# Two layers of a hybrid encoder on one core: where a block's products with the states and the norm's sums stand on TensorE

## The chip, the cores and the metric

The kernel runs on one core of a Trainium2 chip. The metric is the device time of one execution in microseconds (us). A core has TensorE (PE, matrix products; PEld is its weight load), VectorE (DVE), ScalarE (ACT), GpSimd (POOL) and SyncE (SP, which issues nearly all transfers here). They run side by side, each takes its own instructions in order, and they wait for one another through semaphores.

## The reference, cut to what matters

Two layers are computed one after the other on a sequence of 512 tokens of width 1024. In each layer three branches read the same input: a state-space branch (SSD) that runs in both directions, a differential attention, and a cross-attention to 256 memory tokens. Their results are gated, merged, projected, and normalised with the residual. The edit lies in the state-space branch:

```python
def _ssd_scan(xs, a, bm, cm):              # one direction, chunks of 128 tokens
    a_cum = jnp.cumsum(a, axis=-1)
    decay = jnp.exp(jnp.where(lower, seg, -jnp.inf))          # seg = a_cum[q] - a_cum[s]
    y_diag = jnp.einsum('bcqgn,bcsgn,bgrcqs,bcsgrp->bcqgrp', cm, bm, decay, xs)
    states = jnp.einsum('bcqgn,bgrcq,bcqgrp->bcgrpn', bm, decay_states, xs)
    ...                                    # prev: the states carried from chunk to chunk
    y_off = jnp.einsum('bcqgn,bcgrpn,bgrcq->bcqgrp', cm, prev, jnp.exp(a_cum))
    return (y_diag + y_off).reshape(Bsz, L, H, P)
...
    y = y_fwd + y_bwd + d_skip.astype(jnp.float32)[:, None] * xs
    y = y.reshape(Bsz, L, SSD_INNER) * jax.nn.silu(z.astype(jnp.float32))
    return _rmsnorm(y, norm_w)             # over all 2048 channels of a token
```

There are 32 heads of 64 channels in 4 groups of 8 heads, and 4 chunks. A head's output has a part from within its chunk (`y_diag`) and a part from the states of earlier (backwards: later) chunks (`y_off`). The norm needs the sum of squares over all channels of a token, so over all groups.

## The kernel before, in words

**Units of weights.** All weights lie in memory as units of 128x1024 numbers. The list `plan` holds steps, each with or without a unit. `emit` goes through it: for a step with a unit it loads a unit some steps ahead (`wr`, two buffers, issued on SP), ACT rounds it to the short float format (`wh`, three buffers), DVE takes the rest (`wl`), and `proj` multiplies it in 24 matmuls (`mm3`: three for each of eight input tiles) into one bank `pj`. The input's two parts are `xh` and `xl`.

**The state-space branch, `ssd`.** For each group `g` of 8 heads: `bpart` and `cpart` project and convolve B and C (`bC`, `cC`) and form `gs`, the products of B and C within each chunk; four times `xpart` does so for the inputs (`xsC`, and transposed `xsT`); `states` forms the states `prev` carried between the chunks, in both directions. Then come four blocks `b`, each of two heads: `zpart` (a projection, the gate `sz`) and `ypart`. After the first group the `wpart` units, which multiply a group's result `yh`, `yl` with the branch's output weights and add it into `mrg` (`br` in the code), stand among the next group's `xpart` steps; those of the last group follow at the end. Some gates of the other branches are computed ahead between the blocks (`AHEAD`, tile `tg`).

**One block, `ypart`.** In this order it issues
1. two loads of `eb` (the exponentials of the summed decays, spread over the partitions) on SP, two buffers;
2. the products of the states with C for both directions, 6 matmuls `pm<-cC,prev` (12 records in the trace) into two banks `pm`, and on DVE their multiplication into `eb` (`eb<-pm,eb`, two of 128x384);
3. for each of its two heads: a load of `ab` (512 KB, two buffers), a minimum with the mask on DVE, eight exponentials on ACT, a sum on DVE, and the product with `gs`, which gives `m` (three buffers);
4. the products within the chunk, 8 matmuls `pm<-m,xsT` (16 records) into a bank `pm` called `py`;
5. on DVE `y` (first `y<-xsC,pr,pm`, then two additions of `eb`, then the product with `sz`), `yh` on ACT, `yl` on DVE, the square on ACT, and its addition into `sqa` on POOL.

**The order on each engine.** A planner goes through the program as it is written and gives each instruction a number that counts up; on each engine the instruction with the lowest number that it holds to be ready goes next, by its own model of durations. Two helpers change that. Inside `manual_schedule(engines={PE})` PE's instructions keep their written order among themselves, while others may still go between. `late(n)` adds `n` to the number of what stands inside (`late(-n)` takes `n` off), and what is inside doesn't count for what comes after. The first of the 8 matmuls of step 4 stands under `late(LD)`, the others under `late(-LD)` with `LD` = 80: the set is held back by 80 instructions, and once its first matmul has gone, the others follow at once. Tiles of one tag are given out in the order of the program; `pm` has 4 banks.

**The end of the branch.** `gpart(j)` projects the gates of this branch (tiles `th` and `sz`), three of them ahead; `norm` sums `sqa` over the partitions by four matmuls with one column each (`pt<-cst,sqa`, 8 records), takes the reciprocal root on DVE in small steps, spreads it by four matmuls (`pm<-cst,rs_y`), and ACT copies it into `rB`. The four `wpart(3, u)` follow, and then `fin(j)` multiplies gate, `rB` and `mrg`. In the code:

```python
            if j == 1:
                self.T(norm)
        for u in range(4):
            self.T(wpart(3, u), (l, UBS + 12 + u))
```

Of the kernel before, what the change touches and what calls it, by code (L numbers as in the profile page):

```python
# [15 lines left out]
ALU = mybir.AluOpType  # L16
# [4 lines left out]
P = 128  # L21
# [23 lines left out]
LX, LD, LN = 70, 80, 300  # L45
# [6 lines left out]
def bc(ap, shape):  # L52
    return ap.broadcast_to(shape)


class Net:
# [389 lines left out]
    def ssd(self, l):  # L446
# [85 lines left out]
        def ypart(g, b):  # L532
            def f():
                sp = self.sp
                if b == 0:
                    self.yh = self.t(sp, [P, 4, S], "yh", F32R)
                    self.yl = self.t(sp, [P, 4, S], "yl", F32R)

                eb = self.t(sp, [P, 2, S], "eb", bufs=2)
                for hh in range(2):  # L540
                    h = g * 8 + 2 * b + hh
                    src = self.deb.rearrange("(d h) q -> h d q", d=2)[h:h + 1]
                    nc.sync.dma_start(out=eb[hh * 64:(hh + 1) * 64], in_=src.broadcast_to([64, 2, S]))
                for d, cs in ((0, (1, 2, 3)), (1, (0, 1, 2))):
                    ps = self.bank(self.pm, "pm")
                    for c in cs:
                        q = slice(c * P, (c + 1) * P)
                        self.mm(ps[:, q], self.prev[d, c][:, b * P:(b + 1) * P], self.cC[:, q])
                    q = slice(cs[0] * P, (cs[2] + 1) * P)
                    self.tt(eb[:, d, q], ps[:, q], eb[:, d, q], ALU.mult)  # L550

                py = self.bank(self.pm, "pm")
                ms = []
                for hh in range(2):
                    h = g * 8 + 2 * b + hh
                    ab = self.t(sp, [P, 2, 4, P], "ab", bufs=2)
                    src = self.dab.rearrange("(d h) q -> h d q", d=2)[h:h + 1]
                    nc.sync.dma_start(out=ab.rearrange("p d c q -> p d (c q)"), in_=src.broadcast_to([P, 2, S]))

                    self.tt(ab, ab, bc(self.msk[:, :, None, :], [P, 2, 4, P]), ALU.min)  # L560
                    for d in range(2):
                        for c in range(4):
                            j = 32 * d + h
                            self.act(ab[:, d, c, :], ab[:, d, c, :], AF.Exp, bias=self.bias[:, c, j:j + 1])
                    self.tt(ab[:, 0], ab[:, 0], ab[:, 1], ALU.add)
                    m = self.t(sp, [P, 4, P], "m", bufs=3)
                    self.tt(m, ab[:, 0], self.gs, ALU.mult)
                    ms.append(m)
                with self.tc.manual_schedule(engines={mybir.EngineType.PE}):
                    for i in range(8):  # L570
                        c, hh = i // 2, 1 - i % 2
                        e = slice(b * P + hh * 64, b * P + hh * 64 + 64)

                        with self.late(-LD if i else LD):
                            self.mm(py[hh * 64:(hh + 1) * 64, c * P:(c + 1) * P], self.xsT[:, c, e], ms[hh][:, c, :])
                y = self.t(sp, [P, S], "y", bufs=2)
                self.stt(y, self.xsC[b], self.par[:, PDS + 4 * g + b:PDS + 4 * g + b + 1], py, ALU.mult, ALU.add)
                self.tt(y[:, P:], y[:, P:], eb[:, 0, P:], ALU.add)
                self.tt(y[:, :3 * P], y[:, :3 * P], eb[:, 1, :3 * P], ALU.add)
                self.tt(y, y, self.sz, ALU.mult)  # L580
                nw = self.par[:, PNW + 4 * g + b:PNW + 4 * g + b + 1]
                self.act(self.yh[:, b, :], y, scale=nw)
                self.stt(self.yl[:, b, :], y, nw, self.yh[:, b, :], ALU.mult, ALU.subtract)
                sq = self.sz
                self.act(sq, y, AF.Square)
                self.tt(self.sqa, self.sqa, sq, ALU.add, nc.gpsimd)
            return f

        def wpart(g, u):
            def f(wh, wl):  # L590
                yh, yl = self.yhl[g]
                for i in range(2):
                    ps = self.bank(self.pj, "pj")
                    for k in range(4):
                        c = slice(k * 256 + i * P, k * 256 + (i + 1) * P)
                        self.mm3(ps, wh[:, c], wl[:, c], yh[:, k, :], yl[:, k, :], k == 0, k == 3)
                    o = self.br[:, 2 * u + i, :]
                    if g == 0:
                        self.act(o, ps)
                    else:  # L600
                        self.tt(o, o, ps, ALU.add)
            return f
# [21 lines left out]
        def gpart(j):  # L624
            def f(wh, wl):
                self.gt[j] = self.gate(self.sp, wh, wl, 0, j, "th" if j % 4 < 2 else "sz")
            return f

        def fin(j):
            def f():  # L630
                t, o = self.gt.pop(j), self.br[:, j, :]
                self.stt(t, t, 1.0, self.rB, ALU.add, ALU.mult)
                self.tt(o, o, t, ALU.mult)
            return f
# [29 lines left out]
        self.gt = {}  # L664
        for j in range(3):
            self.T(gpart(j), (l, UGL + j))
            if j == 1:
                self.T(norm)
        for u in range(4):
            self.T(wpart(3, u), (l, UBS + 12 + u))  # L670
        for j in range(KC):
            if j + 3 < KC:
                self.T(gpart(j + 3), (l, UGL + j + 3))
            self.T(fin(j))
# [638 lines left out]
```

## Time and profile before

| | us |
|---|---|
| three runs, median | 2211.78 |
| lowest, highest | 2208.17, 2215.52 |
| the profiled execution, its own time | 2208.37 |
| its span, first to last instruction | 2206.5 |
| busy: PE, DVE, ACT, POOL | 2158.8, 1609.6, 1022.9, 52.7 |

The state-space branch lies at about 20 to 500 us in layer 0 and at 1145 to 1650 us in layer 1. The profile's rows name an engine, the line of the code (for matmuls L103, a helper's, and so the tiles tell them apart), output and inputs, and shape. Times are counted from the span's start. A row of the timeline may hold several instructions of one kind (x16). In square brackets stands how long the engine was idle before it, and who ended that. A matmul's end is modelled and overlaps the next one, so the distance from start to start is the better measure of what it takes. The granted clock is the share of full speed that PE's clock had.

### The profile page before, as it was taken

The page shows a single profiled execution, that of the slowest core. Times are in us where ns is not written, and L with a number is a line of the kernel's source. Part 1 is how long each engine was busy: PE and PEld are TensorE (multiplying, and loading weights), DVE is VectorE, ACT ScalarE, POOL GpSimd, SP SyncE. Part 2 cuts the span into 40 slices and gives each one's busy share as a digit, 9 for nine tenths or more (in the row PEclk, how much of TensorE's full clock was granted, in tenths as well). Part 3 has the DMA queues.
Part 4 walks back from the last instruction along what each step waited for, and adds up shares of the span by engine and source line. Part 5 has one row for each costly group of instructions (what it writes and reads, how often), then busy time and mean ns, then how long its engine had stood idle before and what let it go on. Part 6 is the DMA issues. An engine that isn't in the chain of part 4 may idle for free.

```text
span 2206.5 us, 29202 instructions
## 1 busy us (share of the span) xinstructions
PE 2158.8 (98%) x11122; PEld 1780.2 (81%) x11122; DVE 1609.6 (73%) x2486; ACT 1022.9 (46%) x1935; POOL 52.7 (2%) x38
## 2 busy tenths in 40 slices
PE   8999999999999999999999999999999999999998
PEld 6777877778888888887887777777788888888876
DVE  7897888858554778866467887888754547788667
ACT  5664546424432555543345564555423325555430
POOL 0000000000000000000000000000100000000000
PEclk9999999999999999999999999999999999999999
DMA  4654544335553433324564654444434334333253
GB/s 151 172 171 129 157 133 147 111 95 174 164 170 120 134 110 111 108 88 153 157 220 111 169 143 143 143 141 137 120 99 130 111 109 136 111 110 106 90 159 109
DMA packets 109680, 295.27 MB, mean 134 GB/s; under 512 B 12460, under 2 KB 13028, under 8 KB 109284
## 3 DMA queue, kind: packets, MB, share of 16 engines
q1 hardware_dynamic: 109540, 293.41, 44.1%
q8 instruction: 87, 1.43, 0.3%
q14 instruction: 53, 0.43, 0.1%
HBM read 255.06 MB, written 17.33 MB: 123 GB/s over the span
## 4 chain that ended last, share of the span: by engine, by line
PE 76%; DVE 11%; DMA 7%; ACT 3%; issue 2%; POOL 0%; SPq 0%; POOLq 0%; DVEq 0%; ACTq 0%
PE pj L103 59%; PE pm L103 15%; DMA ab<-dab 5%; PE pt L111 2%; DVE ab L81 2%; DVE wl L81 2%; DVE acc L84 2%; DVE y L81 1%; DMA wr<-wu 1%; ACT wh L91 1%; ACT ab L91 1%; DVE yl L84 1%; DVE m L81 1%; DMA fth<-rd 1%; DVE eb L81 1%
## 5 line engine op out<-in xcount | busy, mean ns | idle before, releaser
L103 PE MATMUL pj<-xh,wl 128*128 128x512 f32 x1664 | 663.8, 399 | 5.5 <-ACT mrg L91 3.8
L103 PE MATMUL pj<-xh,wh 128*128 128x512 f32 x1664 | 659.5, 397 | 6.9 <-ACT xh L91 6.0
L103 PE MATMUL pj<-xl,wh 128*128 128x512 f32 x1664 | 658.7, 396 | 0.0
L81 DVE TENSOR_TENSOR wl<-wr,wh 128x1024 fp32r<-128x1024 f32 x330 | 404.8, 1227 | 102.4 <-ACT wh L91 101.9
L91 ACT ACTIVATE wh<-wr 128x1024 fp32r<-128x1024 f32 x330 | 347.3, 1053 | 215.8 <-PE pj L103 139.5
L103 PEld LDWEIGHTS pj<-xh,wh 128*128 128x128 f32 x1664 | 313.5, 188 | 79.1 <-ACT xh L91 6.0
L103 PEld LDWEIGHTS pj<-xh,wl 128*128 128x128 f32 x1664 | 313.6, 188 | 76.5 <-ACT mrg L91 5.5
L103 PEld LDWEIGHTS pj<-xl,wh 128*128 128x128 f32 x1664 | 313.8, 189 | 66.2 <-issue 4.2
L91 ACT ACTIVATE ab<-ab,bias 128x128 f32<-128x128 f32 x512 | 160.7, 391 | 117.9 <-DVE ab L81 116.1
L84 DVE SCALAR_TENSOR_TENSOR acc<-pj,hcw,acc 128x510 f32<-128x510 f32 (+1 forms) x192 | 141.6, 742 | 26.5 <-ACT acc L91 25.5
L941 DVE TENSOR_REDUCE fmx<-pm 128x1 f32<-128x512 f32 x128 | 85.0, 685 | 47.0 <-PE pm L103 47.0
L103 PE MATMUL pj<-yl,wh 128*128 128x512 f32 x256 | 103.8, 406 | 0.8 <-DVE yl L84 0.8
L103 PE MATMUL pj<-yh,wh 128*128 128x512 f32 x256 | 104.4, 408 | 0.0
L103 PE MATMUL pj<-dy,wh 128*128 128x512 f32 (+1 forms) x384 | 102.6, 356 | 1.3 <-DVE dy L81 1.3
L81 DVE TENSOR_TENSOR ab<-ab,cst 128x1024 f32<-128x1024 f32 x64 | 85.7, 1338 | 24.1 <-DMA ab<-dab 24.0
L103 PE MATMUL pj<-yh,wl 128*128 128x512 f32 x256 | 103.2, 404 | 0.1
L91 ACT ACTIVATE fpp<-pm,fmx 128x512 f32<-128x512 f32 x128 | 87.2, 686 | 33.6 <-DVE fmx L941 33.6
L103 PE MATMUL pj<-cy,wh 128*128 128x512 f32 x256 | 78.8, 389 | 0.0
L103 PEld LDWEIGHTS pj<-dy,wh 128*128 128x128 f32 x384 | 67.5, 188 | 13.7 <-DVE dy L81 2.6
L103 PE MATMUL pj<-wh,xl 128*128 128x256 f32 x256 | 73.3, 286 | 0.0
L103 PE MATMUL pj<-wl,xh 128*128 128x256 f32 x256 | 72.4, 283 | 0.0
L103 PE MATMUL pj<-wh,xh 128*128 128x256 f32 x256 | 72.4, 283 | 0.0
(280 smaller groups left out, 3317.2 us busy)
## 6 DMA issues: line engine op xcount, KB each, us to landing
wr<-wu SPq DMA_DIRECT2D x336, 512.0 KB, 3.7
ab<-dab SPq DMA_DIRECT2D x64, 512.0 KB, 5.6
eb<-deb SPq DMA_DIRECT2D x64, 256.0 KB, 4.8
mkv<-dkv SPq DMA_DIRECT2D x16, 512.0 KB, 3.9
rsw<-rx SPq DMA_DIRECT2D x64, 128.0 KB, 2.3
dy<-dy SPq DMA_DIRECT2D x32, 256.0 KB, 2.3
dgt<-tg SPq DMA_DIRECT2D x16, 256.0 KB, 4.2
dkv<-mo SPq DMA_DIRECT2D x16, 256.0 KB, 4.3
```

Of the source, the lines that this page charges most:

```text
L81: (eng or self.nc.vector).tensor_tensor(out=out, in0=a, in1=b, op=op)
L84: self.nc.vector.scalar_tensor_tensor(out=out, in0=a, scalar=s, in1=b, op0=op0, op1=op1)
L91: self.nc.scalar.activation(out=out, in_=a, func=f, **kw)
L103: self.nc.tensor.matmul(out=out, lhsT=a, rhs=b, start=first, stop=last)
L111: self.nc.tensor.transpose(out=out, in_=x, identity=self.ident)
L941: nc.vector.tensor_reduce(out=mx[:, c:c + 1], in_=ps, axis=AX.X, op=ALU.min)
```

## The change

Step 2 of `ypart` is taken from its place and put behind step 4: its 6 matmuls stand inside the same `manual_schedule` block, under `late(-LD)`, and the two multiplications into `eb` follow outside of it, ahead of `y`. The number of instructions, their shapes and the tiles stay. And `norm` no longer stands behind the second gate of the last group, but behind `wpart(3, 0)`, that is behind the third gate and the first output unit.

```diff
-                for d, cs in ((0, (1, 2, 3)), (1, (0, 1, 2))):
-                    ps = self.bank(self.pm, "pm")
-                    for c in cs:
-                        q = slice(c * P, (c + 1) * P)
-                        self.mm(ps[:, q], self.prev[d, c][:, b * P:(b + 1) * P], self.cC[:, q])
-                    q = slice(cs[0] * P, (cs[2] + 1) * P)
-                    self.tt(eb[:, d, q], ps[:, q], eb[:, d, q], ALU.mult)
 
                 py = self.bank(self.pm, "pm")
                 ms = []
...
                         with self.late(-LD if i else LD):
                             self.mm(py[hh * 64:(hh + 1) * 64, c * P:(c + 1) * P], self.xsT[:, c, e], ms[hh][:, c, :])
+
+                    far = ((0, (1, 2, 3)), (1, (0, 1, 2)))
+                    pss = [self.bank(self.pm, "pm") for _ in far]
+                    with self.late(-LD):
+                        for (d, cs), ps in zip(far, pss):
+                            for c in cs:
+                                q = slice(c * P, (c + 1) * P)
+                                self.mm(ps[:, q], self.prev[d, c][:, b * P:(b + 1) * P], self.cC[:, q])
+                for (d, cs), ps in zip(far, pss):
+                    q = slice(cs[0] * P, (cs[2] + 1) * P)
+                    self.tt(eb[:, d, q], ps[:, q], eb[:, d, q], ALU.mult)
                 y = self.t(sp, [P, S], "y", bufs=2)
...
             self.T(gpart(j), (l, UGL + j))
-            if j == 1:
-                self.T(norm)
         for u in range(4):
             self.T(wpart(3, u), (l, UBS + 12 + u))
+            if u == 0:
+                self.T(norm)
```

## The prediction

> **What bounds the kernel now.** I read the page's busy line and its chain first, then what TensorE (PE) waits for, then the granted clock around those waits, and last the order of the two kinds of product on PE.
>
> ```profile
> PE 2158.8 (98%) x11122; PEld 1780.2 (81%) x11122; DVE 1609.6 (73%) x2486; ACT 1022.9 (46%) x1935; POOL 52.7 (2%) x38
> PE 76%; DVE 11%; DMA 7%; ACT 3%; issue 2%; POOL 0%; SPq 0%; POOLq 0%; DVEq 0%; ACTq 0%
> ```
>
> PE is busy 98% of the span and carries 76% of the chain that ended last. So an edit gains what it takes out of PE's idle time, and what it lets PE do faster; work moved on other engines counts where PE then waits. The next view is the waits of PE: total in us, how often, longest.
>
> ```profile
> PE pm L103 <- DVE m L81: 8.3, 8, 2.2
> PE pt L103 <- POOL sqa L81: 4.4, 2, 2.4
> PE pm L103 <- DVE xw L81: 4.4, 2, 2.6
> PE pj L103 <- ACT mrg L91: 3.8, 4, 2.3
> ```
>
> The edit aims at the second row: `norm` sums `sqa` by matmuls, and PE waits there for POOL's last addition, once per layer. The first row is the decay tile `m`, for which a block's products within the chunk wait; its large entries lie in the first group of each layer. The windows add what the waits do to the clock (columns: length, busy time of PE, its weight loads, DVE, ACT and POOL with counts, then the granted clock).
>
> ```profile
> 448.29:451.70 3.41, 1.35 (x10) 1.14 (x10) 0.80 (x2) 2.33 (x4) 1.26 (x1) 1.00 0.21 87
> 451.71:455.12 3.41, 3.41 (x9) 2.63 (x9) 2.50 (x11) 0.00 (x0) 0.00 (x0) 0.50 0.00 0
> 455.13:458.54 3.41, 3.41 (x19) 2.71 (x19) 1.09 (x4) 0.20 (x1) 0.00 (x0) 1.00 0.53 154
> ...
> 1318.70:1322.11 3.41, 3.28 (x8) 2.61 (x9) 2.48 (x5) 3.02 (x7) 0.00 (x0) 0.50 0.52 154
> ...
> 1602.01:1605.42 3.41, 3.41 (x10) 2.65 (x9) 2.45 (x8) 0.00 (x0) 0.00 (x0) 0.50 0.26 48
> 96.00:104.50 8.50, 6.31 (x46) 5.18 (x45) 7.67 (x11) 5.92 (x17) 1.52 (x1) 1.00 0.48 154
> ```
>
> After 3.41 us with 1.35 us of PE work the granted clock is 0.50 for exactly 3.41 us, then 1.00 again; the same stands behind the wait in layer 1 (1602.01) and behind one at 1318.70. The longest wait for `m` lies inside 96 to 104.5 (8.50 less 6.31 busy, 2.2 us) and left the clock at 1.00. So the two waits of `norm` cost more than their idle time.
>
> **The norm's place, term one.** PE rows, start and duration:
>
> ```profile
> 448.11 0.39 PE L103 MATMUL pj<-yh,wl 128*128 128x512 f32 x1
> 450.56 1.05 PE L103 MATMUL pt<-cst,sqa 128*128 128x1 f32 x8 [2.06 <-POOL sqa L81]
> ...
> 452.28 0.63 PE L103 MATMUL pj<-yh,wl 128*128 128x512 f32 x1
> 452.71 0.63 PE L103 MATMUL pj<-yl,wh 128*128 128x512 f32 x1
> ...
> 455.21 0.39 PE L103 MATMUL pj<-yl,wh 128*128 128x512 f32 x1
> 455.44 0.39 PE L103 MATMUL pj<-yh,wh 128*128 128x512 f32 x1
> ...
> 1599.59 1.05 PE L103 MATMUL pt<-cst,sqa 128*128 128x1 f32 x8 [2.38 <-POOL sqa L81]
> ```
>
> Idle: 2.06 + 2.38 = 4.4 us. Slow clock: projection matmuls start 0.43 us apart (452.28, 452.71) instead of 0.23 (455.21, 455.44). The 3.41 us at that spacing hold as many starts as 3.41 x 0.23 / 0.43 = 1.8 us would, so 1.6 us are lost, and as much in layer 1: 3.2 us. In the new order `norm` stands behind the first output unit of the last group, that is 24 matmuls x 0.23 = 5.5 us later than the row at 448.11, and one of these 24 already stands ahead of it. The wait for `sqa` ends at 450.56; PE would come to it at 448.1 + 5.5 = 453.6 even without the edit's other half, so it is covered with 3 us to spare. I take the whole: -4.4 and -3.2.
>
> What is late next? The unit in front reads `yh` and `yl` of the last block in its fourth input tile, its tenth matmul, 9 x 0.23 = 2.1 us after its start. The last block in layer 0, DVE and POOL:
>
> ```profile
> 442.66 0.75 DVE L84 SCALAR_TENSOR_TENSOR y<-xsC,pr,pm 128x512 f32<-128x512 f32 x1
> 444.81 1.23 DVE L81 TENSOR_TENSOR wl<-wr,wh 128x1024 fp32r<-128x1024 f32 x1 [1.40 <-ACT wh L91]
> 445.95 1.15 DVE L81 TENSOR_TENSOR y<-y,eb 128x384 f32<-128x384 f32 x2
> ...
> 448.62 0.75 DVE L84 SCALAR_TENSOR_TENSOR yl<-y,pr,yh 128x512 fp32r<-128x512 f32 x1 [0.79 <-ACT yh L91]
> ...
> 449.25 1.26 POOL L81 TENSOR_TENSOR sqa<-sqa,sz 128x512 f32<-128x512 f32 x1 [11.00 <-ACT sz L91]
> ```
>
> `yl` ends at 448.62 + 0.75 = 449.4. The unit starts at 448.1 and would reach it at 450.2; with the products of term two put ahead (1.3 us), 451.5. If both `eb` multiplications (0.47 us each from start to start, below) are added to this chain, `yl` ends at 450.3. So no new wait, by 1 us at least: the chain stands behind a weight split (444.81) that waited 1.40 us for ACT, and the multiplications fit in that gap. The rest of `norm` (reciprocal root, broadcast, `rB`) moves with it and must be done before the fourth gate's slot is needed; three output units x 5.5 = 16 us of PE work lie between. Its instructions (8 small matmuls on PE, 14 on DVE and ACT) pass two projections and their weight splits; none is a DMA or on POOL, so those two queues keep their order.
>
> **The products with the states, term two.** All 6 matmuls per block stay; they move from ahead of a block's products within the chunk to right behind them. On the trace (12 records are 6 matmuls) blocks 1 to 3 already have theirs behind such a set, but the set of the block before:
>
> ```profile
> 188.89 0.83 PE L103 MATMUL pm<-cC,prev 128*128 128x128 f32 x6
> 189.48 0.48 PE L103 MATMUL pj<-xh,wh 128*128 128x512 f32 x1
> 189.84 0.94 PE L103 MATMUL pm<-cC,prev 128*128 128x128 f32 x6
> 190.53 0.47 PE L103 MATMUL pj<-xh,wl 128*128 128x512 f32 x1
> 190.84 0.39 PE L103 MATMUL pj<-xl,wh 128*128 128x512 f32 x1
> ...
> 197.87 1.60 PE L103 MATMUL pm<-cC,prev 128*128 128x128 f32 x12
> 199.23 0.48 PE L103 MATMUL pj<-xh,wl 128*128 128x512 f32 x1
> ```
>
> Behind a set they take 199.23 - 197.87 = 1.36 us, till the next projection matmul. Block 0's stand alone in two halves: from 188.89 to 190.84 are 1.95 us with two projection matmuls in them, less 2 x 0.23 = 1.49. So the eight first blocks gain 0.13 each at most, 1.0 us; at least nothing (the halves stand behind the states' own products, whose tail they may hide). I take half, -0.5.
>
> What moves with them: DVE's `eb` multiplications wait for PE one block later, and so does the whole chain of `y` in that block. Behind them DVE has the minimum and product of the next heads, for which PE's next set and SP's next `ab` load wait. Today's rows for such a block:
>
> ```profile
> 102.36 0.75 DVE L84 SCALAR_TENSOR_TENSOR y<-xsC,pr,pm 128x512 f32<-128x512 f32 x1 [0.68 <-PE pm L103]
> 103.22 0.56 DVE L81 TENSOR_TENSOR eb<-pm,eb 128x384 f32<-128x384 f32 x1
> 103.69 0.55 DVE L81 TENSOR_TENSOR y<-y,eb 128x384 f32<-128x384 f32 x1
> 104.16 0.55 DVE L81 TENSOR_TENSOR eb<-pm,eb 128x384 f32<-128x384 f32 x1
> 104.62 0.55 DVE L81 TENSOR_TENSOR y<-y,eb 128x384 f32<-128x384 f32 x1
> ```
>
> The two `eb` rows here belong to the next block, the others to this one: same number, same places. With the block's own products in the same place the chain is as long as now, so I count nothing. SP's `eb` loads keep their places and are needed a block later. PSUM: three of the four `pm` banks are held at once, as now.
>
> The price lies at block 0. Its 1.3 us of PE work no longer stand ahead of its set, so PE comes earlier, and waits longer where `m` holds it up. That is in the first groups: the list of PE's waits for 70 to 130 us and for 1215 to 1275 us (7.9 of the 8.3 us in all), and two rows of DVE:
>
> ```profile
> PE pm L103 <- DVE m L81: 3.4, 3, 2.2
> PE pm L103 <- DVE m L81: 4.5, 4, 2.0
> ...
> 1220.78 0.56 DVE L81 TENSOR_TENSOR eb<-pm,eb 128x384 f32<-128x384 f32 x1
> 1221.25 0.69 DVE L81 TENSOR_TENSOR m<-ab,gs 128x512 f32<-128x512 f32 x1
> ```
>
> But `m` comes earlier too: at 1220.78 DVE took `eb` and only then `m` (1221.25), so at least 0.47 us go there. Bounds for each layer: +1.3 us (nothing of it reaches `m`) to -1.0 (two multiplications leave a full DVE and the chain of `ab` loads starts earlier). I take +0.3, twice, as the one row that shows it gives 0.5 of the 1.3 and later waits of the same stage (the fourth row of the waits) absorb part. In the other groups PE waits for `m` 0.4 us in all, and the blocks just move together.
>
> **Sum.** -4.4 - 3.2 - 0.5 + 0.6 = -7.5 us. Against the profiled execution (2208.4 us) that is 2200.9; that execution lies 3.4 us below the median of the three runs (2211.8), so on the median 2204.3, 0.34% less. About 0.3%, 6.6 us, is what can be told from no change here.
>
> [...]
>
> **Rivals.** (1) The slow windows are not these waits' doing and come anyway, as the slow clock appears in other places too: -7.5 + 3.2 = -4.3, 2207.5. For it: the 2.2 us wait for `m` had none. Against: the slow windows of `norm` begin within 3 us of its wait's end in both layers. Chance 0.10. [...]
> (2) The first groups' waits grow by the full 1.3 us per layer and pass the point where the clock halves: 2.2 + 1.3 = 3.5 us. Then -8.1 + 2 x (1.3 + 1.6) = -2.3, 2209.5. For it: 2.2 and 2.0 us, the longest there, are near the 2.3 us (the longest for `mrg`, ahead of 1318.70) that halved it. Chance 0.15.
> (3) The wait comes back at the output unit's fourth tile, for `yl`: the sum of squares is just behind it in the same chain. It needs `yl` 1 us later than worked out; if half of idle and slow clock return, -7.5 + 3.8 = -3.7, 2208.1. Chance 0.06. (4) The planner leaves PE's order as it is, no change, 2211.8: 0.05.
> (5) Slower. DVE takes its instructions in order; if the planner puts both `eb` multiplications ahead of `y`'s first step, as they are written, each block's DVE work stands 1.36 us for the products. In the eight blocks of the two first groups this reaches `m` and PE: 8 x 1.36 = 10.9 us, and four more slow windows 6.4: +17.3 - 8.1 = +9, 2221. It decides from 1 us per block (8.1 / 8). Against: the rows at 102.36 to 104.62, where `y` goes first, as its matmuls end first. Chance 0.07.
>
> **Numbers.** The forecast has 0.57. Its own range is 2200 to 2208 (slow windows at first groups come or one at 1318.70 goes, 1.6 us each; block 0 from -2.0 to +2.6), so about a fifth of it is within 0.3%. Faster 0.46; within 0.47 (0.11 of the forecast, rivals 1 to 4); slower 0.07. The range for all, 2198 to 2212, leaves out rival 5 and the tails.
>
> **What would show it.** Right: the wait of PE for `sqa` is gone from the list; the windows behind it show 1.00; each set of products within the chunk is followed at once by 12 records with the states, none stands alone; `eb` rows lie behind the block's own `y` row. Wrong: a wait of PE for `yl` in the first unit of the last group; waits for `m` above 11 us in all; granted 0.50 in the first groups; DVE idle ahead of `eb`.

## The result and the profile after

The changed kernel takes 2226.3 us in the median of six runs (2222.0 to 2230.8), the kernel before 2210.0 (2203.4 to 2215.5) on the same chip: a ratio of 1.0074, 95% interval 1.0057 to 1.0091. It is slower by 0.7%, and 2204.3 was forecast. The profiled execution has a span of 2226.6 us against 2206.5. In all runs below, the ratio is to the kernel before, run alternately on the same chip; its median was 2207.8 to 2210.0 us in every round, so times of different rounds are also set side by side. One run of 2990 us (new order in the first groups only) and one of 6792 us (the last kernel) are in a slow state and left out of the medians; the expectations written later count the first one in, as 2209.0.

The page of the kernel after, its busy line and the shares of its chain:

```profile
PE 2166.1 (97%) x11122; PEld 1788.6 (80%) x11122; DVE 1601.4 (72%) x2486; ACT 1023.9 (46%) x1935; POOL 60.0 (3%) x38
PE 77%; DVE 10%; DMA 10%; ACT 2%; issue 1%; SPq 0%; DVEq 0%; ACTq 0%
```

PE still bounds the kernel, with as many instructions as before. DMA's share of the chain went from 7% to 10%. What PE waits for (us in all, times, longest):

```profile
PE pt L111 <- DVE bC L84: 14.4, 5, 4.8
PE pm L103 <- DVE m L81: 10.4, 5, 2.7
```

The wait for `sqa` (4.4 us) is gone, as forecast, and only 0.3 us for `yl` (at 466.07, in the first output unit of layer 0) have taken its place. But a wait that was 1.0 us before is now the longest of all: PE stands for `bC`, the convolved B of the next group, which it must transpose. Its four large entries, in PE's timeline, lie at the ends of groups 1 and 2 of both layers:

```profile
244.40 0.66 PE L111 MATMUL pt<-cst,bC 128*128 128x128 f32 x4 [2.06 <-DVE bC L84]
...
356.36 0.90 PE L111 MATMUL pt<-cst,bC 128*128 128x128 f32 x3 [4.31 <-DVE bC L84]
...
1401.76 0.66 PE L111 MATMUL pt<-cst,bC 128*128 128x128 f32 x4 [3.03 <-DVE bC L84]
...
1514.25 1.12 PE L111 MATMUL pt<-cst,bC 128*128 128x128 f32 x4 [4.82 <-DVE bC L84]
```

To see where the time went, take in both traces the start of the first `pm<-xw,bT` of each group (the states' own products) as a mark. The length from mark to mark, in us:

| kernel | layer 0: group 0 to 1 | 1 to 2 | 2 to 3 | layer 1: 0 to 1 | 1 to 2 | 2 to 3 |
|---|---|---|---|---|---|---|
| before | 111.5 | 107.3 | 107.8 | 116.9 | 108.3 | 107.3 |
| after | 116.9 | 109.8 | 113.7 | 119.7 | 110.7 | 113.8 |

Groups 1 and 2 lost 2.5 + 5.8 + 2.4 + 6.5 = 17.2 us, the first groups 5.5 + 2.8 = 8.3 us. The stretch with the norm's sums gained some 2.7 and 4.4, 7.1 in all (in layer 0 it is 2.4 to 3.0, by where one takes its end). With 1.3 us ahead of all of the edit's work and 0.5 between the layers this makes the 20.1 us by which the spans differ. These are two executions, and the first group varies from one to the next: with its old order it took 111.5 to 114.3 us in layer 0 and 112.1 to 116.9 in layer 1 (kernel before, norm alone, and the three below that keep it), so its 8.3 us are rough. Groups 1 and 2 are steadier, 107.3 to 109.2 with the old order.

Why is `bC` late? The order on VectorE (DVE) has changed. Block 1 of group 1, in the kernel before (start, duration, operation) and in the kernel after:

```profile
206.36 0.74 DVE L84 SCALAR_TENSOR_TENSOR y<-xsC,pr,pm 128x512 f32<-128x512 f32 x1
...
208.42 0.55 DVE L81 TENSOR_TENSOR y<-y,eb 128x384 f32<-128x384 f32 x1
208.94 1.23 DVE L81 TENSOR_TENSOR ab<-ab,cst 128x1024 f32<-128x1024 f32 x1
```

```profile
212.13 1.23 DVE L81 TENSOR_TENSOR ab<-ab,cst 128x1024 f32<-128x1024 f32 x1 [1.90 <-DMA ab<-dab]
213.28 0.74 DVE L84 SCALAR_TENSOR_TENSOR y<-xsC,pr,pm 128x512 f32<-128x512 f32 x1
213.93 1.02 DVE L81 TENSOR_TENSOR eb<-pm,eb 128x384 f32<-128x384 f32 x2
214.87 0.55 DVE L81 TENSOR_TENSOR y<-y,eb 128x384 f32<-128x384 f32 x1
```

Before, the minimum over the next heads' `ab` stood behind the first three steps of `y`. Now it stands ahead of all of them, and it has to wait 1.90 us for its load. The set of products that `y` needs began at 210.23 (204.88 before) and by the profile ended at 211.32, but DVE stood idle till 212.13 and took `y` behind the minimum: it starts 3.05 us after the set's start instead of 1.48. In blocks 2 and 3 it is 4.6 and 4.4 us instead of 1.5 and 2.0. One row of the page's groups shows it for the whole kernel (busy, mean ns | idle before, what ended it), before and after:

```profile
L81 DVE TENSOR_TENSOR ab<-ab,cst 128x1024 f32<-128x1024 f32 x64 | 85.7, 1338 | 24.1 <-DMA ab<-dab 24.0
```

```profile
L81 DVE TENSOR_TENSOR ab<-ab,cst 128x1024 f32<-128x1024 f32 x64 | 78.2, 1221 | 52.2 <-DMA ab<-dab 52.1
```

DVE's idle time for these loads has doubled, 24 to 52 us. In groups 1 to 3 (190 to 460 us and 1330 to 1620 us) it was 1.3 and 3.4 us and is 12.9 and 16.9. A block that is late on DVE hands this on to what is queued behind it. At the end of group 1 that is B's convolution:

```profile
239.81 0.74 DVE L84 SCALAR_TENSOR_TENSOR acc<-pj,hcw,acc 128x510 f32<-128x510 f32 x1
240.47 1.22 DVE L81 TENSOR_TENSOR ab<-ab,cst 128x1024 f32<-128x1024 f32 x1
241.60 0.74 DVE L84 SCALAR_TENSOR_TENSOR y<-xsC,pr,pm 128x512 f32<-128x512 f32 x1
...
243.66 0.69 DVE L84 SCALAR_TENSOR_TENSOR bC<-th,acc 128x512 f32<-128x512 f32 x1
```

Between the last step of the sum `acc` and `bC` stand a minimum and the late `y` with its `eb` rows. PE has no more to do ahead of the transposes and waits till 244.40.

Last, the granted clock, in stretches of the kernel after (length, PE, its weight loads, DVE, ACT, POOL, then the clock):

```profile
99.50:102.91 3.41, 1.37 (x7) 0.79 (x5) 3.38 (x4) 3.41 (x12) 0.77 (x1) 1.00 0.10 32
102.92:106.33 3.41, 2.90 (x20) 2.60 (x21) 2.40 (x4) 1.14 (x2) 0.00 (x0) 0.50 0.74 214
106.34:109.74 3.40, 3.40 (x14) 3.04 (x13) 2.00 (x4) 0.00 (x0) 0.00 (x0) 0.50 0.75 214
...
459.00:462.40 3.40, 3.40 (x22) 2.94 (x20) 2.62 (x4) 0.71 (x1) 0.00 (x0) 1.00 0.16 24
```

The slow windows behind the norm are gone (1.00 at 459). But the waits for `m` in the first groups and for `bC` bring their own. Eleven windows of 3.41 us at 0.50 stand in this trace ahead of its last 15 us, five in the one before. At the prediction's 1.6 us each, the six more are an estimated 9.6 of the 20.1 us at most, since PE also waits inside some of them.

### The profile page after: what moved, and what is told of

Its sections match the earlier page's. It is cut to its first block, busy times and chain, and to the rows that moved or that the text cites. A ratio compares the mean times of both kernels' runs of the same rounds, so it can differ in the third digit from the quotient of the medians.

```text
span 2226.6 us, 29197 instructions
## 1 busy us (share of the span) xinstructions
PE 2166.1 (97%) x11122; PEld 1788.6 (80%) x11122; DVE 1601.4 (72%) x2486; ACT 1023.9 (46%) x1935; POOL 60.0 (3%) x38
## 4 chain that ended last, share of the span: by engine, by line
PE 77%; DVE 10%; DMA 10%; ACT 2%; issue 1%; SPq 0%; DVEq 0%; ACTq 0%
PE pj L103 59%; PE pm L103 15%; DMA ab<-dab 6%; PE pt L111 2%; DVE ab L81 2%; DMA wr<-wu 2%; DVE wl L81 2%; DVE y L81 1%; DMA fth<-rd 1%; DVE acc L84 1%; ACT wh L91 1%; DVE eb L81 1%; DVE m L81 1%; DVE y L84 0%; ACT ab L91 0%
## 5 line engine op out<-in xcount | busy, mean ns | idle before, releaser
L81 DVE TENSOR_TENSOR ab<-ab,cst 128x1024 f32<-128x1024 f32 x64 | 78.2, 1221 | 52.2 <-DMA ab<-dab 52.1
L81 POOL TENSOR_TENSOR sqa<-sqa,sz 128x512 f32<-128x512 f32 x32 | 58.8, 1837 | 868.1 <-ACT sz L91 868.1
```

The lines of the kernel that those rows point to most:

```text
L81: (eng or self.nc.vector).tensor_tensor(out=out, in0=a, in1=b, op=op)
```

## The experiments

The reasons on trial, as the expectations name them. **A**: the minimum that waits for its load ahead of `y` on DVE, which makes `bC` late in groups 1 to 3. **B**: the loss is in the first groups. **C**: the norm's move disturbs what follows it. **F**: PE's own new order makes `bC` late. **D**, **E** and **H** are about the first groups, **G** about a means of test.

### Which part, and which groups

Four kernels. The first has the norm's move alone, the second the other move alone. The last two have both moves, but the products with the states stand in the new place only where a condition holds, and in the old place elsewhere. The third has this condition:

```diff
+                if not (g > 0):
+                    for d, cs in ((0, (1, 2, 3)), (1, (0, 1, 2))):
...
-                    far = ((0, (1, 2, 3)), (1, (0, 1, 2)))
+                    if g > 0:
+                        far = ((0, (1, 2, 3)), (1, (0, 1, 2)))
...
-                for (d, cs), ps in zip(far, pss):
+                if g > 0:
+                    for (d, cs), ps in zip(far, pss):
```

In the fourth it is `g == 0`.

Norm alone. Expected: 

> The norm's move alone, the products with the states in their old place. By the stages of the two traces the stretch with the norm's sums became 2.7 us shorter in layer 0 and 4.4 us in layer 1, 7.1 in all. Theory A (the loss is in VectorE's order: in groups 1 to 3 the next heads' minimum, which waits for its load, now goes ahead of a block's first step of y, so B's convolution ends later and TensorE waits for bC): this run is 7 us below the kernel before, about 2203 against 2210, ratio 0.997, no wait for sqa, no wait for bC above 1 us. Rival B (the loss is in the first groups, where nothing stands ahead of block 0's set any more): the same 2203. Rival C (the norm's move itself disturbs what follows it, and the gain of the sqa wait is given back): 2210 or above.

Measured: 2199.9 us, ratio 0.9964 (0.9952 to 0.9977). Two of PE's waits:

```profile
PE pm L103 <- DVE m L81: 7.0, 7, 1.9
...
PE pt L111 <- DVE bC L84: 1.1, 1, 1.1
```

Products alone. Expected: 

> The move of the products with the states alone, the norm in its old place. Theory A: the whole loss of the edit is here and the norm's 7 us come on top: 2226 + 7 = 2233, ratio 1.010; waits for bC of some 14 us in all, in four places of 2 to 5 us. Rival B: the same time, but with most of the added idle time and slow clock between 70 and 130 us and between 1215 and 1290. Rival C: 2210 to 2215, since what was lost came with the norm.

Measured: 2225.9 us, 1.0084 (1.0071 to 1.0098).

```profile
PE pt L111 <- DVE bC L84: 15.4, 5, 5.0
...
PE pt L103 <- POOL sqa L81: 3.2, 2, 2.0
```

New order in groups 1 to 3 only. Expected: 

> Both moves, but the first group of each layer keeps the products with the states in the old place; groups 1 to 3 have the new order. From the traces, stage by stage: groups 1 to 3 lost 2.5 + 5.8 us in layer 0 and 2.4 + 6.5 in layer 1, 17.2 in all, the first groups 5.5 + 2.8 = 8.3. Theory A: 2210 - 7 + 17 = 2220, ratio 1.0045, and the waits for bC stay at about 14 us. Rival B (the loss is in the first groups): 2203 to 2206, ratio 0.997 to 0.998, waits for bC below 2 us.

Measured: 2217.4 us, 1.0045 (1.0031 to 1.0059).

```profile
PE pt L111 <- DVE bC L84: 11.1, 5, 3.7
PE pm L103 <- DVE m L81: 8.0, 7, 1.9
```

New order in the first groups only. Expected: 

> Both moves, but the new order of the products with the states only in the first group of each layer; groups 1 to 3 keep the old one. Theory A: 2210 - 7 + 8 = 2211, ratio 1.000, no wait for bC above 1 us; the waits for m stay near 10 us with slow clock behind them. Rival B: 2220 or more.

Measured: 2208.3 us, 1.0005 (0.9993 to 1.0018).

```profile
PE pm L103 <- DVE m L81: 12.7, 8, 2.6
...
PE pt L111 <- DVE bC L84: 1.5, 2, 1.3
```

C falls: the norm's move alone gains 8.5 us. B falls as the main cause: against the norm alone, groups 1 to 3 cost 2217.4 - 2199.9 = 17.5 us and the first groups 2208.3 - 2199.9 = 8.4, close to the 17.2 and 8.3 of the marks. The second kernel missed A's figure: 2233 was expected, and it took no more than with the norm moved. Its wait for `sqa` was 3.2 us, with one slow window (at 462) instead of two. So what the norm's move is worth depends on the order ahead of it. With the products moved it can't be told from nothing.

### Giving `y` its place back

The products with the states stay in their new place. Two operations of one column, a multiplication of the first step of `y` by zero and an addition, make the minimum of the second head in blocks 2 and 3 depend on the first step of the last `y`. This is called the tie (32 multiplications and 12 additions in the program).

```diff
+                    if hh and g > 0 and b > 1:
+                        self.tt(ab[:, 0, 0, :1], ab[:, 0, 0, :1], self.ty, ALU.add)
                     self.tt(ab, ab, bc(self.msk[:, :, None, :], [P, 2, 4, P]), ALU.min)
...
                 self.stt(y, self.xsC[b], self.par[:, PDS + 4 * g + b:PDS + 4 * g + b + 1], py, ALU.mult, ALU.add)
+                self.ty = self.t(sp, [P, 1], "ty", bufs=2)
+                self.ts(self.ty, y[:, :1], 0.0, ALU.mult)
```

Expected: 

> The changed kernel, and in groups 1 to 3 the minimum of a block's second head is made to depend on the first step of y of the block before, by two additions of one column (VectorE, 24 of each; the added number is zero). TensorE's order stays that of the changed kernel; VectorE's goes back to y ahead of the next heads' minimum. Theory A (the minimum that waits for its load at the head of VectorE's queue is the cause): the waits for bC fall from 14 us to 2 at most, the first step of y follows its set by 1.4 to 2 us again instead of 3 to 7, and the 17 us of groups 1 to 3 come back: 2226 - 17 = 2209, ratio to the kernel before 1.000. Rival F (TensorE's own order is the cause: 1.4 us of products behind each set, B's transposes four projection matmuls nearer): the waits for bC stay, 2223 to 2227, ratio 1.006 to 1.008.

Measured: 2204.5 us, 0.9990 (0.9975 to 1.0004), 22 us below the kernel after. PE's waits, and DVE at the place shown above (block 1 of group 1):

```profile
PE pm L103 <- DVE m L81: 11.3, 10, 3.4
...
PE pt L111 <- DVE bC L84: 1.2, 1, 1.2
```

```profile
212.02 0.74 DVE L84 SCALAR_TENSOR_TENSOR y<-xsC,pr,pm 128x512 f32<-128x512 f32 x1
...
214.13 0.15 DVE L81 TENSOR_TENSOR ab<-ab,ty 128x1 f32<-128x1 f32 x1
214.20 1.22 DVE L81 TENSOR_TENSOR wl<-wr,wh 128x1024 fp32r<-128x1024 f32 x1
215.34 0.55 DVE L81 TENSOR_TENSOR y<-y,eb 128x384 f32<-128x384 f32 x1
215.81 1.22 DVE L81 TENSOR_TENSOR ab<-ab,cst 128x1024 f32<-128x1024 f32 x1
...
238.78 0.68 DVE L84 SCALAR_TENSOR_TENSOR bC<-th,acc 128x512 f32<-128x512 f32 x1
239.48 0.75 DVE L84 SCALAR_TENSOR_TENSOR y<-xsC,pr,pm 128x512 f32<-128x512 f32 x1
```

The minimum stands behind `y` again and waits for nothing, its load having landed meanwhile. In groups 1 to 3 the first step of `y` follows its set by 1.1 to 1.9 us, and DVE's waits for `ab` loads (190 to 460 us and 1330 to 1620 us) fall from 12.9 and 16.9 us to 1.0 and 0.3. The wait for `bC` is 1.2 us, and from mark to mark groups 1 and 2 take 107.5, 107.3, 107.5 and 107.3 us.

But the tie moved more than the minimum. At the end of group 1 `bC` now goes ahead of block 3's `y` (last two rows), where it stood behind it in the kernel before and in the kernel after. TensorE's order isn't quite the changed one either, against what was expected: in groups 1 and 2 the set of block 3 stands five projection matmuls later, and B's transposes follow right behind it and its products with the states, with no projection matmul between (11 in the kernel after, 15 before). F falls even so: the products with the states stand directly behind each set as in the kernel after, the transposes come nearer still, and nothing is lost. So the loss lies in DVE's order. How much of it is the minimum's wait ahead of `y`, and how much that `bC` stands behind the late `y`, this kernel doesn't separate.

The 22 us are 4 more than the 17.5 that groups 1 to 3 cost. The next kernel shows that the first groups cost 4.8 us here (2204.5 - 2199.7) instead of 8.4; why is open.

The same with the old order in the first groups. Expected: 

> As the run before, but the first group of each layer keeps the old order (the norm moved, groups 1 to 3 in the new order with the tie). Theory A: nothing of the loss is left, so the time is that of the norm's move alone, 2200, or up to 0.5 us less for the lone halves; ratio 0.996. Rival F: 2217, ratio 1.004, as without the tie.

Measured: 2199.7 us, 0.9961 (0.9946 to 0.9976): the norm's gain is whole, and nothing can be seen of the lone halves' 0.5 us. Against the same kernel without the tie (2217.4) this is 17.7 us, the whole loss of groups 1 to 3.

The tie on the old order, as a control (norm moved, no products moved). Expected: 

> Control of the tie: the norm moved, all products with the states in the old place, and the tie in groups 1 to 3. VectorE has y ahead of the minimum there anyway. Theory A: the tie gives nothing by itself, 2199 to 2202 (2199.9 without it), ratio 0.996 to 0.997. Rival G (the tie is a gain of its own, which covered a loss of the new order that is still there with it): 5 to 17 us less, 2183 to 2195, ratio below 0.994.

Measured: 2203.4 us, 0.9974 (0.9963 to 0.9985). G falls. The tie is no gain of its own; it may cost some 3 us (the time is 1.4 us above A's range), though the interval overlaps that of the kernel without it.

### The first groups

The norm moved, and the new order in some blocks of the first groups alone (the condition above with `b == 0`, with `b > 0`, and with `b in (0, 3)`).

Block 0. Expected: 

> The norm moved, and the new order in block 0 of the first group of each layer alone. With all four blocks of the first groups in the new order the time was 9 us above the norm's move alone (2209.0 against 2199.9). Theory D (in each block of a first group VectorE now stands for the products with the states, whose two multiplications go ahead of the next heads' minimum): block 0 has a quarter of it at most, 2200 to 2202, ratio 0.996 to 0.997. Rival E (block 0's set comes 1.3 us earlier and waits for m, as the prediction had it): the whole 9 us, 2207 to 2209, ratio 0.9995.

Measured: 2196.4 us, 0.9948 (0.9927 to 0.9968), below the figures of both.

Blocks 1 to 3. Expected: 

> The norm moved, and the new order in blocks 1 to 3 of the first group of each layer alone; block 0 keeps the old one. Theory D: three quarters of the 9 us or more, 2206 to 2209, ratio 0.999 to 1.000, waits for m near 12 us. Rival E: 2200 to 2202, waits for m near 7 us.

Measured: 2206.8 us, 1.0001 (0.9985 to 1.0016), waits for `m` 12.9 us in all.

So E falls as the prediction had it: block 0, the only block that I had priced, loses nothing there. The loss is in the blocks behind. D's times fit, but in the second of these kernels DVE waits for the products ahead of `eb` for only 1.0 us (70 to 140 us) and 2.1 us (1205 to 1295), too little for 7 to 10. (In the kernel after it is 1.6 and 1.5 us.) Next, the whole change with the tie in all groups. Expected: 

> The changed kernel with the tie in all groups, the first ones too (blocks 2 and 3 of every group, and block 0 of groups 1 to 3). In the first groups of the changed order VectorE waits for ab loads at the head of its queue for 8.2 us (layer 0) and 10.4 us (layer 1), against 5.1 and 4.8 with the old order. Theory A (these waits are the first groups' loss as well): they fall to some 5 us each, and of the 4.8 us between the tie in groups 1 to 3 (2204.5) and the old first groups (2199.7) most comes back: 2199 to 2202, ratio 0.996 to 0.997. Theory D (VectorE stands for the products with the states in the first groups): the tie does nothing for that, 2204 to 2206, ratio 0.998 to 0.999.

Measured: 2205.4 us, 0.9990 (0.9977 to 1.0003): nothing gained over 2204.5. That is D's figure, though the waits that D names are too short, as said above. DVE's waits between 1205 and 1295 us, in the kernel with the new order in the first groups alone and in this one:

```profile
DVE ab L81 <- DMA ab<-dab: 10.4, 5, 2.7
```

```profile
DVE ab L81 <- DMA ab<-dab: 7.8, 4, 2.8
```

The tie took part of the waits for loads away and no time came back, so A as I had it doesn't explain the first groups. Last, block 3 beside block 0. Expected: 

> The norm moved, and the new order in blocks 0 and 3 of the first groups alone (block 0 alone: 2196.4; blocks 1 to 3: 2206.8). If the first groups' loss is in blocks 1 and 2, where a minimum that waits for its load now also stands ahead of the sum over the two directions of the head before (theory A in another form): 2196 to 2198, ratio 0.995. If it is in block 3, after which B's convolution and the output units of the group follow (theory H: with its products behind the set, the additions of y and with them yh and yl come later): 2203 to 2207, ratio 0.998 to 1.000.

Measured: 2207.0 us, 0.9992 (0.9979 to 1.0004), H's figure, 10.5 us above block 0 alone. In this one step the change on DVE is plain to see. It comes a block earlier, in block 2 (layer 0), whose own products stand in the old place in both kernels; block 0 alone first, then with block 3:

```profile
115.13 0.75 DVE L84 SCALAR_TENSOR_TENSOR y<-xsC,pr,pm 128x512 f32<-128x512 f32 x1
116.00 0.56 DVE L81 TENSOR_TENSOR eb<-pm,eb 128x384 f32<-128x384 f32 x1
116.47 0.55 DVE L81 TENSOR_TENSOR y<-y,eb 128x384 f32<-128x384 f32 x1
116.94 0.55 DVE L81 TENSOR_TENSOR eb<-pm,eb 128x384 f32<-128x384 f32 x1
117.40 0.55 DVE L81 TENSOR_TENSOR y<-y,eb 128x384 f32<-128x384 f32 x1
```

```profile
114.67 0.75 DVE L84 SCALAR_TENSOR_TENSOR y<-xsC,pr,pm 128x512 f32<-128x512 f32 x1
115.33 1.22 DVE L81 TENSOR_TENSOR ab<-ab,cst 128x1024 f32<-128x1024 f32 x1
116.47 0.55 DVE L81 TENSOR_TENSOR y<-y,eb 128x384 f32<-128x384 f32 x1
119.56 1.23 DVE L81 TENSOR_TENSOR ab<-ab,cst 128x1024 f32<-128x1024 f32 x1 [2.54 <-DMA ab<-dab]
120.71 0.55 DVE L81 TENSOR_TENSOR y<-y,eb 128x384 f32<-128x384 f32 x1
```

The `eb` rows of block 3 stood between the dependent steps of block 2's `y`. With block 3's products moved they are gone from there, and the planner has put the two minimums of the next heads in their places. The second one waits 2.54 us for its load, and the last addition of `y` comes at 120.71 instead of 117.40. How much of the 10.5 us this is, and how much comes from PE reaching block 3's set 1.4 us earlier (it waits 2.4 us for `m` there, with a slow window behind), was not taken apart. The two traces differ by 12.6 us in the first groups. Counted by the same projection matmul, 2.0 us of that in layer 0 and 4.2 in layer 1 arise at block 3's set; most of the rest lies at waits that stand in both traces, where a slow window fell in the second alone. Blocks 1 and 2 alone were not tried. So the first groups' loss comes with the blocks behind block 0, with block 3 beside block 0 enough for it, but its cause is open between A in this form, E at block 3, and H.

### The version that the runs point to

Norm moved, block 0 of the first groups in the new order, groups 1 to 3 in the new order with the tie. Expected: 

> The version that the runs point to: the norm moved; in the first groups the new order in block 0 alone (2196.4 without more); in groups 1 to 3 the new order with the tie (2199.7 against 2199.9 without it). If the two add, 2196 to 2197, ratio 0.995; if block 0's 3.5 us were only where the slow clock happened to fall, 2199 to 2200, ratio 0.996.

Measured: 2194.3 us, 0.9944 (0.9924 to 0.9964): faster than both kernels, by 0.6% and some 1.4%. Block 0 alone (2196.4) and the norm alone (2199.9) can't be told from it by their intervals, so only the norm's move, 8.5 us, is shown as a gain.

## Why the prediction was wrong

- **The norm's place** (-4.4 and -3.2): right for the old order. Alone it gains 8.5 us where 7.6 were worked out. The wait and both slow windows went, and for `yl` PE waited 0.3 us, in layer 1. But it doesn't simply add to the other move, as the sum has it: with the products moved the kernel takes 2226.3 us with the norm's move and 2225.9 without.
- **The products with the states, PE's part** (-0.5): nothing seen, 2199.7 against 2199.9. It is too small to be measured here.
- **What moves with them on DVE: the step that failed.** "The two `eb` rows here belong to the next block, the others to this one: same number, same places. With the block's own products in the same place the chain is as long as now, so I count nothing." The number is the same, but the places are not equal. The next block's `eb` rows don't depend on this block's `y`, and filled the gaps between its dependent steps. The block's own rows both go ahead of the additions, and the gaps are open for whatever the planner holds to be ready: `m`, and the minimums. In group 1 the traces show `m` one place earlier and a minimum ahead of `y`. That the earlier `m`, which frees the buffer for the next load, is why the planner moved the minimum is argued, not shown. On the chip the load lands up to 3.1 us after DVE has come to it. The term was 0 and measured 17.5 us in groups 1 to 3. The tie, which puts `y` ahead of the minimum again and in block 3 also `bC` ahead of `y`, removes all of it.
- **"In the other groups PE waits for `m` 0.4 us in all, and the blocks just move together"**: wrong in the same way. I looked only at the wait that was there. What was queued behind `y` at the group's end, B's convolution, had 1.0 us of waits before and was priced nowhere. There was hardly any cover there: in the kernel before, `bC` ended at 236.25 and PE began its transposes at 236.38, so nearly all that makes it later is paid.

```profile
235.57 0.68 DVE L84 SCALAR_TENSOR_TENSOR bC<-th,acc 128x512 f32<-128x512 f32 x1
```

```profile
236.38 0.60 PE L111 MATMUL pt<-cst,bC 128*128 128x128 f32 x4
```

- **The first groups** (+0.6, with -1.0 to +1.3 per layer): measured +8.4 for both, far outside. The term was put on block 0, which loses nothing; the loss is behind it.
- **Rival 5** had the right sign and the right engine, DVE standing in its queue ahead of `y`, at 2221. It had the wrong instruction (the `eb` multiplications instead of a minimum behind a load), the wrong groups for the larger part (17.5 us against 8.4), and a chance of only 0.07. I set it aside because today's order shows `y` ahead of `eb`. That order was the planner's answer to a program that the edit changes.
- **Rival 2 and the signs.** What rival 2 named came as well: the first groups' waits for `m` grew from 7.9 to 10.4 us, and behind three of them the clock halved, for four windows (two from 102.92, one each from 1242.97 and 1273.69), where it had not before. But they didn't grow at block 0, where the rival had it: with block 0 alone in the new order they are 6.1 us. Of the signs of being wrong, these windows and DVE idle ahead of `eb` (3.1 us in the first groups) were seen; `m` waited 10.4 us in all, below the 11 named, and the wait for `yl` was 0.3 us. The wait that cost most, for `bC`, was not among the signs.

## What to carry to other kernels

Where a planner sets the order, moving instructions on one engine changes what fills the gaps on the others: list, for each gap between dependent steps, what fills it now and what is ready to fill it once that is gone. An instruction that waits for a load was a bad filler on DVE here, since what stood behind it waited too (idle time for the `ab` loads 52 us instead of 24). A false dependency of one column can change such an order (here it brought back 17.7 to 22 us), but look at what else the planner then moves. And price a wait by the stage's end, by what is queued behind the late chain, not by the waits that the profile before happens to show.

## What the runs showed of the hardware

In each trace the slow windows lie on a grid: they begin at multiples of 3.413 us from one another, at an offset that differs between executions (1.15 us into the span before, 0.52 after). So I counted PE's idle time in every window of that grid, over 14 traces (some 8,800, the first 20 and last 15 us left out; windows that were slow themselves aren't counted). With 1.93 us idle or more, 45 of 45 were followed by a slow one; with 1.84 to 1.93, 11 of 16; with 1.70 to 1.84, none of 8; below that nine in all, six of them at one place where two short waits with transposes between them fall together (1140 to 1155 us, at the end of layer 0; 0.74 and 0.88 us in the kernels before and after) and two at the norm's sums, whose matmuls have one column each. The kernels before and after alone: 10 of 10 with 1.93 us or more, none of one with 1.84 to 1.93, none of three with 1.70 to 1.84, and three of the nine below. Two waits of the kernel after show the difference:

```profile
352.10:355.50 3.40, 0.00 (x0) 0.00 (x0) 3.08 (x5) 3.20 (x9) 0.00 (x0) 1.00 0.07 29
355.51:358.92 3.41, 2.56 (x8) 2.23 (x9) 3.41 (x7) 2.02 (x6) 0.00 (x0) 0.50 0.15 37
...
536.41:539.82 3.41, 1.59 (x14) 1.39 (x12) 1.07 (x2) 1.13 (x2) 0.00 (x0) 1.00 0.68 231
539.83:543.24 3.41, 3.17 (x14) 2.64 (x15) 3.38 (x6) 1.25 (x2) 0.00 (x0) 1.00 0.47 179
```

The wait of 4.31 us that ends at 356.36 fills a whole window, and the clock halves. One of 2.06 us at 538.0 lies across a border, 1.82 us in the first window (3.41 - 1.59) and the rest in the next, and costs no clock. The wait of 2.06 us for `sqa` in the kernel before lay within one window and did; that of 2.38 us in layer 1 lay across a border, with 0.99 us idle in the window right ahead of the slow one, and did as well (it is one of the two at the norm's sums). So a wait of about 2 to 3.7 us mostly costs 1.6 us more or nothing, by chance of the offset (an estimate: 1.6 from the starts 0.43 and 0.23 us apart, 3.7 as twice the 1.84), which is one source of the spread of some 10 us between runs of one kernel (argued from the traces; the offset of a run without a profile isn't known).
